# A hybrid attention and retention step: the decay table's load, the order of the output projection's first product, and the place of its row sums are changed

## The chip, the cores and the metric

The kernel runs on one core of a Trainium2 chip. The metric is the device time of one execution in microseconds; a kernel's time is the median of its runs. The engines are named as in the profile: PE is TensorE (matmuls; its weight loads are PEld), DVE is VectorE, ACT is ScalarE, POOL is GpSimd, SP is SyncE. SP, ACT and POOL issue DMAs, each on a queue of its own.

## What is computed

One layer of a streaming encoder, for a prompt of 1024 frames and for 8 running streams of 16 new frames each. All data are float32. Cut to what matters:

```
h = rms_norm(x, norm_pre)                                  # 2048 wide
q_sb|k_sb|v_sb|gate_sb|q_r|k_r|v_r|gate_r = h @ w_in       # 8 parts of 8 heads x 128
# group A, stick-breaking attention, per head, strictly causal
z = q k^T / sqrt(128);  a = sigmoid(z) * prod_{later keys} sigmoid(-z);  o_sb = a v
# group B, retention, per head: rotary q and k, chunks with a decay table `intra`
scores = (q k^T) * intra
o_r = scores v + (q S) * decay_read
S   = S * gamma^n + k^T (decay_write * v)
# merge
y = concat(head_rms_norm(o_sb) * silu(gate_sb), head_rms_norm(o_r) * silu(gate_r))
x = x + rms_norm(y @ w_out, norm_post)
```

The samples attend to a cache of 1024 past keys and values per stream, and start from a given retention state. Keys, values and states are returned as well.

## The kernel before, in words

Every large product is made in two parts per operand: `split` makes a rounded high part (ACT, line 166) and the rest (DVE, line 167), and three matmuls (high x high, high x low, low x high) stand for one.

**Groups and heads.** Frames are handled in two groups: group 0 is prompt tiles 0 to 3 and the samples (640 columns, in pieces of 256 and 384), group 1 is prompt tiles 4 to 7 (512 columns). For each group, `for h in range(H)` goes through eight heads. A head makes its value and gate rows (`rows`, matmuls on line 443) and four column projections (keys and queries of the retention, queries and keys of the attention; matmuls on line 386). The weights come in blocks of 256 KB through tile `wr`.

**Jobs and ticks.** The dependent work of a head is written as generators, the jobs: `ret_branch` (retention), `sb_branch` (attention), `decode` (the samples' attention over the cache), and others. After every matmul of a projection the builder calls `tick()`: a clock advances by one (0.75 for a matmul of the rows), and one job that is due is taken one step further, which issues its next instructions at that place of every engine's order. A job's `yield n` asks for the next step n ticks later. So the constants `D_...` at the top of the file set where a job's instructions stand among the matmuls; where a constant is a pair, the first is for group 0. `drain(job)` runs ticks with no matmul between them until the job is finished. Each engine works through its own order; a scheduler places instructions, and `tied` and `pin` keep a DMA or an operation behind the matmul at which it was written (`tied` in group 0 alone).

**The retention's branch.** `ret_branch` writes the keys (`rk`) to DRAM (`turn_out`, line 629), waits `D_TO` ticks, reads them back in turned blocks into `ro` with four DMAs on SP's queue (`turn_in`, line 636), waits `D_TI` ticks, transposes them on DVE (`rkn`, line 1012), and calls `retention`. That loads the head's decay table `dT` (line 887, 128 KB, SP's queue) and at once makes the first scores: a matmul (line 892), a product with `dT` on DVE (`sc`, line 894), and the matmul with the values (line 910). `dT` has one buffer.

**The attention's branch.** `sb_branch` does its scores per tile of 128 frames (line 742), sigmoids, a running product on DVE (line 672), the turning through DRAM on POOL's queue (`be`), a transposition (line 732), and the product with the values (line 769). Both branches end in `Out.finish`: norm, `turn_out`, `D_TO` ticks, `turn_in` on SP's queue, `D_TI` ticks, transposition on DVE (line 707), gain (708), and the store to a scratch tensor `s_y[group][branch and head]` (709).

**The decode.** `decode` (one per head of group 0) loads eight tiles `kcT` of 512 KB on POOL's queue, `D_ZC` ticks apart, then eight tiles `vc` of 512 KB on SP's queue. The two kinds share six buffers (`V_BUFS`). The value products (line 868) are in two sets of four tiles, `D_VC[1]` ticks apart; between them the last two `vc` tiles are loaded into buffers that the first set freed.

**The output projection** is a Strassen-like scheme of seven products (numbers 1 to 7), each with two halves `nh` of 512 output columns and eight blocks `k` of 128 contraction rows. `weights_of` gives a block's weights, some of them sums that were made ahead (`sum_weights`, scratch `s_b`); `left` and `left_sample` load and split the other operand from `s_y` or from row sums `s_s` (`sum_rows`, run by `sums` with a pace `D_SUM2` or `D_SUM3`). `product` makes one half for the accumulators asked for: two for group 0, two for group 1, one for the samples; `collect` adds the results up. Product 5 of group 0 and the samples comes first, while the last head's branches are still running. Then both branches are drained, the buffers of the first stage are given back, and the second stage begins: group 1's operand of product 1 (`yr`) is loaded, and product 1 runs for both groups, group 0 two blocks ahead of group 1 (`LAG`). The eight row sums of group 1 are made there too (`more`).

Of the kernel before, what the change touches and what calls it, by code (L numbers as in the profile page):

```python
# [11 lines left out]
F32 = mybir.dt.float32  # L12
# [6 lines left out]
P = 128  # L19
D = 2048  # L20
KT = D // P
H = 8
# [14 lines left out]
D_ZP = (2, 2)  # L37
D_Z0 = (19, 11)
D_AV = (9, 11)
D_ZC = 24  # L40
D_ROW = 18
D_VC = (6, 46)
V_BUFS = 6
D_RET = (9, 5)
D_TO = (32, 23)
D_TA = (14, 0)
D_TB = (17, 24)
D_TI = (32, 13)
D_OUT = 4
V_SET = 4  # L50
D_SUM = 6
D_TD = 7
D_OFF = 3
N_READ = 40
D_FIN = 2
D_MR = 6
D_OP = 2
D_SUM2 = (4, 6, 28)
D_SUM3 = (3, 3, 6)
MR = 3  # L60
LAG = 2
AHEAD = 2
HT = KT // 2
HALF = D // 2
# [23 lines left out]
def tile_hybrid_step(  # L88
# [368 lines left out]
    with ExitStack() as s1:  # L457
# [424 lines left out]
            oT = op.tile([P, P], F32, name="doT", tag="doT", bufs=1)  # L882
            Job(out.finish(0, 0, h, 4, oT, s_y[0][h][:, 4 * P : 5 * P]))

        def retention(gi, g, h, out, rq, rk, rkn, rv):
            dT = op.tile([P, 2, P], F32, name="dT", tag="dT", bufs=1)
            tied(nc.sync.dma_start(dT, c_dt[:, h]))

            def scores(i, kind):
                bs = slice(i * P, (i + 1) * P)  # L890
                ps = score_tile("rs")
                nc.tensor.matmul(ps[:, :P], rk[:, bs], rq[:, bs], start=True, stop=True)
                sc = op.tile([P, P], F32, name="sc", tag="sc")
                nc.vector.tensor_tensor(sc, ps[:, :P], dT[:, kind, :], ALU.mult)
                return sc

            S = None
            if gi == 1:
                S = op.tile([P, P], F32, name="S", tag="S", bufs=3)
                nc.sync.dma_start(S, s_S[h])  # L900
            sc = scores(0, 0)
            yield D_RET[phase[0]]
            for i in range(4):
                nxt = None
                if i < 3:
                    nxt = scores(i + 1, 0)
                elif SAMPLE in g["tiles"]:
                    nxt = scores(4, 1)
                po = acc_tile()
                nc.tensor.matmul(po[:, :P], sc, rv[:, i, :], start=True, stop=True)  # L910
# [12 lines left out]
                yield D_RET[phase[0]]  # L923
                pS = score_tile("pS")
                nc.tensor.matmul(pS[:, :P], rkn[:, i, :], rv[:, i, :], start=True, stop=True)  # L925
                Sn = op.tile([P, P], F32, name="S", tag="S", bufs=3)
                if S is None:
                    nc.vector.tensor_copy(Sn, pS[:, :P])
                else:
                    nc.vector.scalar_tensor_tensor(  # L930
                        Sn, S, math.exp(LOG_GAMMA[h] * P), pS[:, :P], ALU.mult, ALU.add
                    )
                S = Sn
                sc = nxt
                yield D_RET[phase[0]]
            nc.scalar.dma_start(s_S[h] if gi == 0 else s_prompt[0, 0, h], S)
            if SAMPLE in g["tiles"]:
                yield from sample_retention(h, out, sc, rq, rkn, rv)
# [62 lines left out]
        def ret_branch(gi, g, h, rows_in, rk):  # L1001
# [2 lines left out]
            rkn = ep.tile([P, 6, P], F32, name="rkn", tag="rkn")  # L1004

            out = Out(nt, "ro")
            s = turn_out(rk[:, : nt * P].rearrange("p (k t) -> p k t", t=P), f"s_rk{gi}_{h}")
            yield D_TO[phase[0]]
            raw = out.o.rearrange("p k d -> p (k d)")
# [6 lines left out]
            nc.vector.tensor_scalar(rkn[:, :4, :], rkn[:, :4, :], dec[:, h, 1:2], None, ALU.mult)  # L1016
            while "rq" not in rows_in:
                yield 3
            yield from retention(gi, g, h, out, rows_in["rq"], rk, rkn, rv)
# [23 lines left out]
        def kept(i):  # L1043
            return [[half[i][:, h // 2, h % 2 * 256 : h % 2 * 256 + 256] for h in range(HT)] for half in mov]

        def first_sample():
            mine["s", 0] = [[half[h // WQ][:, h % WQ, NB_TOK:] for h in range(HT)] for half in mov]
            return left_sample(0, *mine["s", 0], wp, "mr", MR)
# [8 lines left out]
        for gi, g in enumerate(GROUPS):  # L1057
# [6 lines left out]
            for h in range(H):  # L1064
                rows_in = {}

                def rows():
                    if (gi, h) == (1, H - 1):
                        sampled.append(Job(first_sample(), 1))
                    rows_of_head(g, mov, h, None if h else loads)  # L1070
                    if h == 0:
                        nc.sync.dma_start(roots[:, :NB_TOK], s_root)
                        rooted_tables(ropes, g["pieces"])
# [124 lines left out]
            return wh, wl  # L1198

        made = collections.deque()  # L1200
        order_of = iter([(n, nh, k) for n in (5, 1, 2, 5, 3, 6, 7) for nh in range(2) for k in range(HT)] + [(4, 0, k) for k in range(HT)])

        def product(n, nh, groups, sample, ticks, upto=HT, feed=(), lag=0):
            todo = [((g, p), bank(), mine[g, n], TS[p]) for g in groups for p in range(2)]
            if sample:
                todo.insert(2, ("s", bank(), mine["s", SAMPLE_LEFT[n]], TS[0]))
            blocks = []
            for k in range(upto + lag):
                if k < upto:
                    made.extend(load_split(*at) for at in itertools.islice(order_of, AHEAD + 1 - len(made)))  # L1210
                    blocks.append(made.popleft())
                next(iter(feed), None)
                for key, a, x, ts in todo:
                    at = k - lag if key[0] == 1 else k
                    if 0 <= at < upto:
                        times(a, x, at, ts, *blocks[at], at == 0, at == HT - 1)
                        for _ in range(ticks):
                            tick()
            return [(key, a) for key, a, _, _ in todo]

        outs, finishing = {}, {}
# [30 lines left out]
        nxt = Job(left(0, 1, *mine[0, 1], wp, "mr", MR), D_OP)  # L1252
        Job(collect(5, 1, product(5, 1, (0,), True, D_OUT)), 1)
        drain(nxt)
        drain(ret_job)
        drain(sb_job)
        while jobs:
# [2 lines left out]
    with ExitStack() as s3:  # L1260
# [107 lines left out]
                yield 30  # L1368

        (first,) = both(1, G1)  # L1370
        more = Job(sums(fp, [sum_rows(1, h) for h in range(H)], D_SUM3, 3), 30)
        Job(load_gpost(), 40)
        ready = [Job(left_sample(1, *mine["s", 1], fp, "ys", 4), 24)]
        for p in range(4):
            outs[1, p] = rp.tile([P, D], F32, name=f"out{p}", tag=f"out{p}")
        for n, groups in ((1, BOTH), (2, BOTH), (5, G1), (3, BOTH), (6, BOTH), (7, BOTH)):
            for nh in range(2):
                if n > 1 and nh == 0:
                    all_of(ready)
# [166 lines left out]
```

## Time and profile before

| | |
|---|---|
| median of 3 runs | 2297.95 us (2295.87 to 2303.42) |
| the profiled execution | 2302.5 us |
| its span, first to last instruction | 2300.8 us |
| granted TensorE clock, mean | 0.989 |
| PE busy | 2232.6 us (97%), 12002 matmuls |
| DVE, ACT, POOL busy | 1252.0, 908.4, 347.9 us |
| DMA | 462.84 MB, mean 201 GB/s |

Times are microseconds from the start of the span. A row of the timeline has start, duration, engine, line, operation, output and inputs, shape, the count of merged instructions, and in brackets the idle time of the engine before it with what ended it. The profile names for that the last event seen; where that had long been over, it was another, often a DMA. "x4" merges instructions of one kind that follow each other. Rows of windows give, after the stretch and its length, the busy time and count of PE, PEld, DVE, ACT and POOL, then the granted clock, the DMA engines' share and GB/s.

### The profile page before, as it was taken

How to read it: one execution, taken by the hardware profiler on the slowest of the kernel's cores; microseconds unless marked ns; L12 is line 12 of the kernel's file. 1: busy time of each engine (PE TensorE's matmuls, PEld its weight loads, DVE VectorE, ACT ScalarE, POOL GpSimd, SP SyncE). 2: the span in 40 equal slices, each digit the busy share in tenths (PEclk: the TensorE clock that was granted, in tenths of full speed). 3: DMA queues.
4: the chain of work that ended last, by engine and by line, in shares of the span. 5: the costliest groups of instructions: out<-in, count | busy, mean ns of one | idle time of the engine just before them, and what ended most of it. 6: DMA issues, size and time to landing. Idle time of an engine off the chain costs nothing.

```text
span 2300.8 us, 34562 instructions
## 1 busy us (share of the span) xinstructions
PE 2232.6 (97%) x12002; PEld 1896.4 (82%) x12002; DVE 1252.0 (54%) x2692; ACT 908.4 (39%) x1963; POOL 347.9 (15%) x577
## 2 busy tenths in 40 slices
PE   8999899999999999999989999999999999799998
PEld 7888889798888979888768888888888887688886
DVE  5335444354444545446556665756666657456567
ACT  6433232333323333334424343443433445335363
POOL 0022030111202021120202111120212113000020
PEclk9999999999999999999999999999999999899999
DMA  8566566574656658467668887887888757665585
GB/s 283 177 201 187 168 186 192 168 226 156 188 166 184 197 162 237 148 199 244 197 196 225 240 224 236 233 232 220 228 236 234 205 148 196 192 208 187 147 218 175
DMA packets 437743, 462.84 MB, mean 201 GB/s; under 512 B 182336, under 2 KB 298048, under 8 KB 437056
## 3 DMA queue, kind: packets, MB, share of 16 engines
q1 hardware_dynamic: 315328, 300.16, 44.7%
q0 software_dynamic: 28720, 78.41, 12.4%
q10 hardware_dynamic: 93520, 82.07, 11.3%
q8 instruction: 94, 1.54, 0.3%
q14 instruction: 81, 0.66, 0.1%
HBM read 359.58 MB, written 110.36 MB: 204 GB/s over the span
## 4 chain that ended last, share of the span: by engine, by line
PE 83%; DMA 8%; issue 3%; DVE 3%; ACT 2%; SPq 1%; ACTq 0%; DVEq 0%; POOL 0%; POOLq 0%
PE accm L443 34%; PE acc L386 26%; PE a L1177 5%; PE a L1181 5%; PE a L1180 5%; PE pa L769 3%; DMA so<-s_o 2%; PE z L742 2%; PE zc L807 1%; DMA ro<-s_rk 1%; SPq L636 1%; PE pa L910 1%; DMA wr<-w_cols 1%; PE pS L925 1%; PE pd L868 1%
## 5 line engine op out<-in xcount | busy, mean ns | idle before, releaser
L386 PE MATMUL acc<-mh,wh 128*128 128x256 f32 (+2 forms) x1536 | 452.4, 345 | 11.4 <-ACT wh L166 10.4
L443 PE MATMUL accm<-whn,mh 128*128 128x512 f32 x1152 | 453.0, 394 | 1.3 <-DVE qs L1128 1.3
L443 PE MATMUL accm<-wln,mh 128*128 128x512 f32 x1152 | 451.0, 391 | 0.5 <-DVE wln L167 0.5
L443 PE MATMUL accm<-whn,ml 128*128 128x512 f32 x1152 | 450.8, 391 | 0.0
L386 PE MATMUL acc<-ml,wh 128*128 128x256 f32 (+2 forms) x1536 | 446.4, 341 | 0.0
L386 PE MATMUL acc<-mh,wl 128*128 128x256 f32 (+2 forms) x1536 | 445.8, 341 | 0.0
L166 ACT ACTIVATE wh<-wr 128x512 fp32r<-128x512 f32 x376 | 237.0, 633 | 467.6 <-PE acc L386 204.8
L167 DVE TENSOR_TENSOR wl<-wr,wh 128x512 fp32r<-128x512 f32 x376 | 257.3, 688 | 289.3 <-ACT wh L166 276.4
L167 DVE TENSOR_TENSOR wln<-wrn,whn 128x512 fp32r<-128x512 f32 x256 | 175.8, 689 | 311.8 <-ACT whn L166 295.8
L166 ACT ACTIVATE whn<-wrn 128x512 fp32r<-128x512 f32 x256 | 161.3, 632 | 404.5 <-PE accm L443 269.2
L386 PEld LDWEIGHTS acc<-mh,wh 128*128 128x128 f32 x1536 | 283.9, 191 | 32.1 <-ACT wh L166 11.9
L386 PEld LDWEIGHTS acc<-ml,wh 128*128 128x128 f32 x1536 | 286.4, 191 | 21.8 <-issue 3.7
L386 PEld LDWEIGHTS acc<-mh,wl 128*128 128x128 f32 x1536 | 285.9, 191 | 21.8 <-issue 1.2
L443 PEld LDWEIGHTS accm<-whn,mh 128*128 128x128 f32 x1152 | 216.3, 188 | 47.2 <-issue 2.5
L443 PEld LDWEIGHTS accm<-wln,mh 128*128 128x128 f32 x1152 | 216.5, 188 | 44.7 <-DVE wln L167 1.3
L443 PEld LDWEIGHTS accm<-whn,ml 128*128 128x128 f32 x1152 | 216.4, 188 | 44.3
L636 POOL DMA_DIRECT2D be<-s_be x128 | 94.1, 741 | 132.9 <-DMA s_be<-be 110.6
L672 DVE TENSOR_TENSOR_SCAN kp<-kp 128x1152 f32<-128x1152 f32 (+4 forms) x40 | 82.4, 2059 | 37.1 <-POOL kp L661 22.6
L661 POOL TENSOR_SCALAR_AFFINE_SELECT kb<-kb 128x128 f32<-128x128 f32 x64 | 35.8, 572 | 411.8 <-ACT kb L655 410.7
L1177 PE MATMUL a<-wh,mh 128*128 128x512 f32 x240 | 94.2, 393 | 3.1 <-ACT kp L655 2.6
L794 POOL DMA_DIRECT2D kcT<-cache_k x64 | 34.6, 544 | 401.7 <-PE pd L868 207.9
L1181 PE MATMUL a<-wh,ml 128*128 128x512 f32 x240 | 94.1, 392 | 0.0
(265 smaller groups left out, 2974.8 us busy)
## 6 DMA issues: line engine op xcount, KB each, us to landing
wr<-w_cols SPq DMA_DIRECT2D x256, 256.0 KB, 4.4
wrn<-w_rows SPq DMA_DIRECT2D x256, 256.0 KB, 3.6
kcT<-cache_k POOLq DMA_DIRECT2D x64, 512.0 KB, 7.4
vc<-cache_v SPq DMA_DIRECT2D x64, 512.0 KB, 5.1
wr<-s_b SPq DMA_DIRECT2D x80, 256.0 KB, 3.9
br<-w_out SPq DMA_DIRECT2D x64, 256.0 KB, 4.7
s_b<-br ACTq DMA_DIRECT2D x32, 512.0 KB, 5.2
wr<-w_out SPq DMA_DIRECT2D x48, 256.0 KB, 3.6
```

The source lines that it names most:

```text
L166: nc.scalar.activation(hi, src, AF.Copy),
L167: nc.vector.tensor_tensor(lo, src, hi.bitcast(F32), ALU.subtract),
L386: last = nc.tensor.matmul(a[:, :m], lhs[:, j, :], rhs[w][:, j, o : o + m], start=(w == 0 and j == 0 and n == 0), stop=(w == KT // WQ - 1 a ...
L443: anchor[0] = nc.tensor.matmul(banks[t], lhs[q][:, j, ts], rhs, start=(k == 0 and n == 0), stop=(k == KT - 1 and n == 2),)
L636: q.dma_start(raw[32 * i : 32 * i + 32, :].rearrange("p (k a) -> p k a", a=32), s[:, :, 32 * i : 32 * i + 32].rearrange("k (j b) a -> b (k ...
L661: nc.gpsimd.affine_select(blk, blk, pattern=[[-1, P]], base=0, channel_multiplier=1, compare_op=ALU.is_gt, fill=fill,)
L672: nc.vector.tensor_tensor_scan(rev, rev, rev, 1.0, ALU.mult, ALU.bypass)
L742: nc.tensor.matmul(z[:, :c], q2[a][:, i * P : (i + 1) * P], k2[b][:, s : s + c], start=(m == 0), stop=(m == 2),)
L769: nc.tensor.matmul(po[:, :P], at[:, j, :], rest["vn"][j], start=(j == 0), stop=(j == t))
L1177: ins = nc.tensor.matmul(a, hi[k][:, ts], wh, start=first, stop=False)
L1180: nc.tensor.matmul(a, hi[k][:, ts], wl, start=False, stop=False)
L1181: anchor[0] = nc.tensor.matmul(a, lo[k][:, ts], wh, start=False, stop=last)
```

## The change

- The load of `dT` is written in `ret_branch` just before `turn_out` instead of at the start of `retention`.
- Constants: `D_ZC` 24 to 23, `D_VC` (6, 46) to (6, 36), `D_TI` (32, 13) to (36, 13), `D_OUT` (ticks per three matmuls in product 5) 4 to 3, `D_SUM2` (4, 6, 28) to (4, 6, 26).
- Product 1 is made by groups. Its first half for group 0 and the samples follows product 5 in the first stage, ahead of the draining of the branches, with `D_OUT` ticks. Its second half for them comes first in the second stage, while group 1's operand is loaded (`feed`). Then both halves for group 1. Its weight blocks are loaded and split twice; `lag` and `upto` are gone.
- Six of the eight row sums of group 1 (`EARLY`) are made by a job of the last head, `early_sums`, behind the sums that `summed` makes; two stay in the second stage.

```
-D_ZC = 24
+D_ZC = 23
-D_VC = (6, 46)
+D_VC = (6, 36)
-D_TI = (32, 13)
-D_OUT = 4
+D_TI = (36, 13)
+D_OUT = 3
+EARLY = 6
-D_SUM2 = (4, 6, 28)
+D_SUM2 = (4, 6, 26)
-LAG = 2
...
-        def retention(gi, g, h, out, rq, rk, rkn, rv):
-            dT = op.tile([P, 2, P], F32, name="dT", tag="dT", bufs=1)
-            tied(nc.sync.dma_start(dT, c_dt[:, h]))
+        def retention(gi, g, h, out, rq, rk, rkn, rv, dT):
...
             out = Out(nt, "ro")                       # in ret_branch
+            dT = op.tile([P, 2, P], F32, name="dT", tag="dT", bufs=1)
+            tied(nc.sync.dma_start(dT, c_dt[:, h]))
             s = turn_out(rk[:, : nt * P].rearrange("p (k t) -> p k t", t=P), f"s_rk{gi}_{h}")
...
+        def early_sums():
+            while not summed[0].done:
+                yield 4
+            yield from sums(ip, [sum_rows(1, h) for h in range(EARLY)], D_SUM2, 2)
...
                     if (gi, h) == (1, H - 1):
                         sampled.append(Job(first_sample(), 1))
+                        Job(early_sums(), 8)
...
-        order_of = iter([(n, nh, k) for n in (5, 1, 2, 5, 3, 6, 7) ...
+        order_of = iter([(n, nh, k) for n in (5, 1, 1, 2, 5, 3, 6, 7) ...
...
-        def product(n, nh, groups, sample, ticks, upto=HT, feed=(), lag=0):
+        def product(n, nh, groups, sample, ticks, feed=iter(())):
             todo = [((g, p), bank(), mine[g, n], TS[p]) for g in groups for p in range(2)]
             if sample:
                 todo.insert(2, ("s", bank(), mine["s", SAMPLE_LEFT[n]], TS[0]))
+            for k in range(HT):
+                made.extend(load_split(*at) for at in itertools.islice(order_of, AHEAD + 1 - len(made)))
+                block = made.popleft()
+                next(feed, None)
                 for key, a, x, ts in todo:
+                    times(a, x, k, ts, *block, k == 0, k == HT - 1)
+                    for _ in range(ticks):
+                        tick()
...
         Job(collect(5, 1, product(5, 1, (0,), True, D_OUT)), 1)
         drain(nxt)
+        Job(collect(1, 0, product(1, 0, (0,), True, D_OUT)), 1)
         drain(ret_job)
         drain(sb_job)
...
-        more = Job(sums(fp, [sum_rows(1, h) for h in range(H)], D_SUM3, 3), 30)
+        more = Job(sums(fp, [sum_rows(1, h) for h in range(EARLY, H)], D_SUM3, 3), 30)
...
-        for n, groups in ((1, BOTH), (2, BOTH), (5, G1), (3, BOTH), (6, BOTH), (7, BOTH)):
+        Job(collect(1, 1, product(1, 1, G0, True, 2, first)), 1)
+        for _ in first:
+            pass
+        for n, groups in ((1, G1), (2, BOTH), (5, G1), (3, BOTH), (6, BOTH), (7, BOTH)):
...
-                start = dict(feed=first, lag=LAG) if (n, nh) == (1, 0) else {}
-                accs = product(n, nh, groups, n < 4, {1: 2, 7: 2}.get(n, 1), **start)
+                accs = product(n, nh, groups, n in (2, 3), {1: 2, 7: 2}.get(n, 1))
```

More of the change, by code (lines that the diff above doesn't have):

```diff
@@ L1018, in ret_branch @@
                 yield 3
-            yield from retention(gi, g, h, out, rows_in["rq"], rk, rkn, rv)
+            yield from retention(gi, g, h, out, rows_in["rq"], rk, rkn, rv, dT)
             yield from out.finish(1, gi, h, 0, rk, s_y[gi][H + h])
@@ L1200, in tile_hybrid_step @@
         made = collections.deque()
-        order_of = iter([(n, nh, k) for n in (5, 1, 2, 5, 3, 6, 7) for nh in range(2) for k in range(HT)] + [(4, 0, k) for k in range(HT)])
-        def product(n, nh, groups, sample, ticks, upto=HT, feed=(), lag=0):
+        order_of = iter([(n, nh, k) for n in (5, 1, 1, 2, 5, 3, 6, 7) for nh in range(2) for k in range(HT)] + [(4, 0, k) for k in range(HT)])
+        def product(n, nh, groups, sample, ticks, feed=iter(())):
             todo = [((g, p), bank(), mine[g, n], TS[p]) for g in groups for p in range(2)]
@@ L1206, in product @@
                 todo.insert(2, ("s", bank(), mine["s", SAMPLE_LEFT[n]], TS[0]))
[L1207 to L1212, printed above, removed]
-                for key, a, x, ts in todo:
[L1214 to L1218, printed above, removed]
+            for k in range(HT):
+                made.extend(load_split(*at) for at in itertools.islice(order_of, AHEAD + 1 - len(made)))
+                block = made.popleft()
+                next(feed, None)
+                for key, a, x, ts in todo:
+                    times(a, x, k, ts, *block, k == 0, k == HT - 1)
+                    for _ in range(ticks):
+                        tick()
             return [(key, a) for key, a, _, _ in todo]
```

## The prediction

> **What bounds the kernel now.** I read the page first, then the waits of TensorE, then the stretch around each large wait (timeline, windows), then the landing times of the transfers in it.
>
> ```profile
> span 2300.8 us, 34562 instructions
> PE 2232.6 (97%) x12002; PEld 1896.4 (82%) x12002; DVE 1252.0 (54%) x2692; ACT 908.4 (39%) x1963; POOL 347.9 (15%) x577
> ...
> PE pa L910 <- DVE sc L894: 18.0, 8, 5.8
> PE a L1177 <- ACT ah L166: 9.8, 1, 9.8
> PE pa L769 <- DVE kp L732: 5.8, 5, 4.3
> ...
>   PE pa L910: 17.3, 7
> DMA to landing us min/median/max: 3.2/8.6/9.9
> ```
>
> TensorE is busy 97% of the span, and the change takes no matmul away, so what can be won is its idle time (2300.8 - 2232.6 = 68.2 us) and the time that it runs at half clock. The waits (us in total, times, longest) name two places. The last two lines are the answer on the tile dT, cut to 0:1065 us (group 0): 17.3 of the 18.0 us fall there, in seven heads, and the decay table takes 8.6 us to land in the median.
>
> ```profile
> 623.17 1.93 PE L868 MATMUL pd<-vc,kp 128*32 128x256 f32 x32
> 636.09 1.93 PE L868 MATMUL pd<-vc,kp 128*32 128x256 f32 x32
> 637.24 2.20 POOL L794 DMA_DIRECT2D kcT<-cache_k  x4 [11.10 <-PE pd L868]
> 637.67 2.42 SPq L636 DMA_DIRECT2D so<-s_o  x4
> 640.14 3.63 SPq L887 DMA_DIRECT2D dT<-c_dt  x1
> 641.00 0.85 DVE L1012 STREAM_TRANSPOSE rkn<-ro 128x640 f32<-128x640 f32 x1
> ...
> 649.93 0.71 DVE L707 STREAM_TRANSPOSE kT<-so 128x512 f32<-128x512 f32 x1 [3.70 <-DMA wrn<-w_rows]
> 650.88 0.49 PE L910 MATMUL pa<-vv,sc 128*128 128x128 f32 x2 [3.40 <-DVE sc L894]
> ...
> DMA to landing us min/median/max: 2.5/9.9/10.6
> DMA to landing us min/median/max: 2.8/9.7/10.4
> ...
> q0 software_dynamic: 576, 2.10, 54.9%
> q1 hardware_dynamic: 3239, 0.89, 34.7%
> ```
>
> This is head 4 of group 0. The second set of value products (636.09) frees four buffers, and POOL at once loads four cache_k tiles of 512 KB into them (637.24). In 637:649 us they move 2.10 MB on POOL's queue, while SyncE's queue gets 0.89 MB. Under that burst lie the attention's turned rows (so, landing in up to 10.6 us; the ro line below it is the retention's) and dT. VectorE works in order: the transposition L707 sits ahead of L894 and waits for so until 649.93, then L894 runs, and TensorE has stood 3.40 us. The name "wrn" in that row is the last event seen, not the cause: so was issued at 637.67 to 639.2, and 639.2 + 10.6 is 649.8. In head 1 it is dT itself:
>
> ```profile
> 243.39 0.49 DVE L894 TENSOR_TENSOR sc<-rs,dT 128x128 f32<-128x128 f32 x2 [4.29 <-DMA dT<-c_dt]
> 243.74 0.79 PE L910 MATMUL pa<-vv,sc 128*128 128x128 f32 x2 [5.79 <-DVE sc L894]
> 916.49 0.49 PE L910 MATMUL pa<-vv,sc 128*128 128x128 f32 x2 [2.08 <-DVE sc L894]
> ...
> 241.80:248.60 6.80, 4.86 (x19) 4.86 (x20) 3.48 (x8) 2.59 (x6) 0.00 (x0) 0.50 0.79 280
> 385.10:388.50 3.40, 3.40 (x16) 3.40 (x16) 1.67 (x5) 1.43 (x4) 0.00 (x0) 0.50 0.60 161
> ...
> 917.60:921.00 3.40, 3.40 (x16) 3.40 (x15) 1.48 (x4) 1.44 (x4) 0.00 (x0) 0.50 0.31 104
> ```
>
> The windows rows (stretch, TensorE busy first, granted clock third from the end) show a second price: four of the seven stalls are followed by 0.50 clock, the first for 6.8 us and three for 3.40 us (first and last shown). Half of the busy time in them is lost: (4.86 + 3 x 3.40) / 2 = 7.5 us.
>
> ```profile
> 1954.22 0.39 PE L1181 MATMUL a<-wh,ml 128*128 128x512 f32 x1
> ...
> 1958.93 3.55 PE pa L769 x16
> 1973.23 2.02 DMA s_y<-so
> 1975.45 5.12 DMA yr<-s_y
> ...
> 1954.50:1981.20 26.70, 12.10 (x54) 10.06 (x53) 6.42 (x19) 4.03 (x12) 2.18 (x4) 0.83 0.43 126
> 1981.20:2029.80 48.60, 48.60 (x205) 40.09 (x206) 30.02 (x71) 23.84 (x53) 0.00 (x0) 0.95 0.80 262
> ```
>
> The second place is the end of the last branches. Output product 5 ends at 1954.22 + 0.39; the last attention head still has one product to do (L769, 1958.93, after a wait of 4.3 us, the longest of its kind above), then its norm, its turning through DRAM and its store (1973.23); group 1's operand (yr) can only be read behind that, and TensorE stands until 1981.2. In 1954.5:1981.2 it is idle 26.70 - 12.10 = 14.6 us, and product 1 runs to 2029.8.
>
> **The change part by part.** A tick is one step of the planner. First and second set of value products are 46 ticks apart in the order written, and 636.09 - 623.17 = 12.92 us: 0.28 us a tick in group 0.
>
> *Decay table (L887).* One 128 KB load per head on SyncE, no more and no fewer, moved from the retention's start to its opening, D_TO + D_TI = 68 ticks or 19 us earlier, past the turn-out (ACT's queue) and the four turn-ins of ro on SyncE's. It delays those by one issue and 128 KB. 19 us exceed the longest landing (9.9), so dT stops being a cause. Its buffer is free: the last head's retention is drained before.
>
> *D_ZC 24 to 23, D_VC's second 46 to 36, D_TI 32 to 36.* Decode up to its second set of value products took 8x24+18+32+32+7+6+46 = 333 ticks, and takes 8x23+18+32+36+7+6+36 = 319: 14 earlier, 3.9 us. The burst so begins near 633.3 in head 4. L707 and L894 come 4 ticks (1.1 us) later. What lies under the burst hence has 5.0 us more before it is asked for; the stalls of heads 2 to 6 are 3.4 us at most. What is late next: ro, whose fourth turn-in is issued at 637.3 and would now lie under the burst. Its transposition L1012 runs at 641.00; but TensorE only runs dry at 650.88 - 3.40 = 647.48, and L1012 to L894 are some 2 us of work, so ro may be about 4 us late for nothing. The nearer set also wants its last two value tiles 2.8 us sooner, 10.1 us after the first set, hardly more than
>
> ```profile
> DMA to landing us min/median/max: 3.7/5.2/9.3
> ```
>
> their longest landing (answer on vc up to 1165 us): no stall, just. Recoverable are 17.3 + 7.5 = 24.8 us. I leave 0.9 us a head for so and ro, 6.3 us, too short for the clock to drop: **gain 18.5 us** (bounds 24.8, and 8 if two thirds of the stalls stay).
>
> *Product 1 by groups.* Its 10 accumulators x 8 blocks x 3 matmuls stay. Group 0 and the samples (3 of 5 accumulators) go first, one half behind product 5 and one behind the branches' end, 144 matmuls; then group 1. From the windows above, without idle time and half clock the stretch would shrink by 14.6 + 0.05 x 48.6 = 2.4, and by half of the 3.55 us of L769 at 1958.93, 1.8 (sixteen such small matmuls elsewhere take half): 18.8 us. Against it:
> - Its 16 weight blocks are loaded and split twice: 4.2 MB, and on ACT and VectorE
>
> ```profile
> L167 DVE TENSOR_TENSOR wl<-wr,wh 128x512 fp32r<-128x512 f32 x15 | 10.4, 691 | 9.5 <-ACT wh L166 8.1 <-DMA yr<-s_y 1.5
> L167 DVE TENSOR_TENSOR al<-yr,ah 128x256 fp32r<-128x256 f32 x15 | 6.2, 421 | 1.5 <-ACT ah L166 1.5
> 238.00:243.70 5.70, 0.00 (x0) 0.00 (x0) 1.37 (x6) 0.00 (x0) 0.00 (x0) 0.83 1.06 363
> 2000.00:2029.00 29.00, 29.00 (x129) 24.02 (x129) 18.34 (x43) 14.57 (x31) 0.00 (x0) 1.00 0.88 290
> ```
>
>  each. A matmul takes 29.00 / 129 = 0.225 us; group 1's half has 48 of them, 10.8 us. In the second one also product 2's operands are made: VectorE 8 x 0.691 + 16 x 0.421 = 12.3 us; DMA 2.1 + 2.1 MB, 11.6 us at the 363 GB/s of that row, 14.5 us at 290. TensorE waits 0.8 to 3.7 us; I take 2.5, as product 2's last blocks can wait.
> - yr waits for the branches' last store, and on SyncE the weights from group 0's fourth block of the second half on stand behind yr: three blocks are made ahead, 27 x 0.225 = 6 us of cover, against 5.1 us for a load at that place. I take 1 us (0 to 4).
> - The last L769 now lies among product 1's matmuls, and L732 ahead of it behind their splits: 0.5 us (0 to 4.3, the stall of now).
>
> *D_OUT 4 to 3* stretches the branches' ticks in products 5 and 1; the 72 more ticks in product 1's first half take it up: 0, covered by group 0's second half, 16 us; without that cover it is the 9.8 us of now.
>
> *Row sums.* Six of eight go from the stage of products 1 and 2 to the last head: the same loads, four VectorE operations and one store each on ACT's queue. They go behind the weight sums, which end sooner as 28 becomes 26, and VectorE is half idle there. 0.5 us.
> Product 1: 18.8 - 4.5 = **14.3 us**.
>
> *Elsewhere.* The last decode is drained at group 1's first head, where its shorter course saves about 1 us. In group 1 dT is not tied and already early: nothing. D_SUM2 moves the loads of the weight sums (br) against the retention's turn-in; in one head they now fall into its midst:
>
> ```profile
> 1567.01 1.20 SPq L278 DMA_DIRECT2D br<-w_out  x2
> ...
> 1575.01 0.71 DVE L1012 STREAM_TRANSPOSE rkn<-ro 128x512 f32<-128x512 f32 x1 [3.10 <-DMA ro<-s_rk]
> 1576.34 0.80 PE L925 MATMUL pS<-vv,rkn 128*128 128x128 f32 x2 [2.33 <-DVE rkn L1016]
> ```
>
> With the half clock behind it, 3.4 us, that is 4.0 us in one head; it may go or come again: 0, within 4.
>
> **Sum.** 18.5 + 14.3 + 1 = 33.8 us. The profiled execution took 2302.5 us with its 1.7 us around the span, 4.55 above the median of 2297.95. 2302.5 - 33.8 = 2268.7 profiled, **2264 us as a median**.
>
> The rule against the row for the clock: the Trainium skill, TensorE: Matmul & The Clock Gate, section HAM oscillation, wants no idle gap above about 3.4 us and lets shorter ones pass. By that rule only the stalls of 5.79 and 3.40 us would cost clock, 4.1 us and not 7.5, and the median would come out at 2267. The trace differs: 0.50 stands behind a stall of 2.08 us (917.60:921.00).
>
> **The rivals.**
> 1. *The stall changes its name.* The burst now lies on ro, and L1012 waits where L894 did. For it: ro's 9.7 us median landing is already long before the burst touches it. Against it: TensorE's 4 us of slack. Two thirds of the stalls stay, group 0 gives 8: 2297.95 - 23.3 = 2275. The Trainium skill, DMA: Bandwidth & Descriptors, section Queues, rings and completion order, says that each engine takes turns between queues packet by packet; by that rule small rows starve beside big ones wherever the burst lies, and the trace agrees (2.10 against 0.89 MB).
> 2. *Group 1's halves become the bound* through DMA and splits, and the weights stand behind yr: product 1 gives 5. For it: 363 GB/s is as much as any row here shows. 2297.95 - 24.5 = 2273.
> 3. *Slower: the weight sums' loads fall on the turn-in in all seven remaining heads of group 1*, and each costs what head 1 of group 0 paid, 5.79 + 4.86 / 2 = 8.2 us: 57 us, 2264 + 57 = 2321. It decides from (33.8 + 6.9) / 7 = 5.8 us a head. Against it: the meeting above cost 4.0.
> 4. *It doesn't do what it says*: the burst follows other waits of POOL, dT stays late behind blocked loads, and group 1's halves return what idle time gives: 2298.
>
> **How the numbers follow.** Forecast 0.54 (2264, its own range 2255 to 2272), rival 1 0.20, rival 2 0.15, rival 3 0.06, rival 4 0.05. All gains at once, 24.8 + 18.8 + 2 + 4 = 49.6, would give 2248; both rivals 1 and 2 give 2284. The range 2251 to 2288 leaves out rivals 3 and 4 and the last of the best case. Faster by over 0.3% (6.9 us, what a measurement of this kernel can tell): 0.89; within 0.05; slower 0.06.
>
> **What would show it.** In the waits, L910's 18.0 us down to 6 or less, dT landing long before L894, and the cache_k loads some 4 us ahead of their place against the second project of the head. Clock of 1.00 around 242, 385, 651 and 918 us. Between product 5 and group 1's first matmul no wait near 9.8 us, group 0's 144 matmuls in one run. Wrong would make it: L1012 waiting for ro in group 0, TensorE waiting for wh in group 1's halves, or L925 waiting in several heads of group 1.

## The result, and the profile after

| | before | after |
|---|---|---|
| median of 20 runs each | 2299.95 us | 2293.28 us |
| the profiled execution | 2302.5 us | 2289.7 us |
| its span | 2300.8 us | 2288.0 us |

The ratio of the times is 0.9969, with a 95% interval of 0.9961 to 0.9977: the change makes the kernel 6.7 us faster. The prediction had the direction (faster) and not the size: 2264, with a range to 2288, where 2293.3 came out. The two profiled executions differ by 12.8 us, nearly twice what the medians do: the one before lies 2.6 us above its median and the one after 3.6 below. So single stages are compared over several kernels below.

The page after (span and busy time), and TensorE's waits (us in total, times, longest):

```profile
span 2288.0 us, 34700 instructions
PE 2228.4 (97%) x12002; PEld 1889.0 (83%) x12002; DVE 1261.5 (55%) x2708; ACT 920.6 (40%) x1981; POOL 344.2 (15%) x577
...
PE acc L386 <- ACT wh L166: 19.8, 3, 9.4
PE a L1182 <- issue: 6.4, 1, 6.4
PE a L1182 <- ACT wh L166: 4.6, 3, 3.4
PE pa L907 <- DVE sc L891: 2.7, 4, 1.3
```

The retention's lines are now up to 3 lower (910 is 907, 894 is 891, 1012 is 1011) and the product's 1177 is 1182; in the experiments some differ by one or two from these. Of the two waits that the prediction went for, the wait for sc fell from 18.0 to 2.7 us and the 9.8 us wait ahead of group 1's product became 6.4. Two new ones stand beside them: 9.4 us for a weight block (L386) in head 1 and 3.4 us for wh in the product.

Head 4 of group 0, the head shown of before, in the timeline of POOL, SyncE and VectorE:

```profile
631.54 2.14 POOL L794 DMA_DIRECT2D kcT<-cache_k  x4 [9.05 <-PE pd L868]
635.14 6.30 SPq L636 DMA_DIRECT2D so<-s_o  x4
642.56 0.84 DVE L1011 STREAM_TRANSPOSE rkn<-ro 128x640 f32<-128x640 f32 x1 [0.96 <-DMA ro<-s_rk]
...
645.28 0.70 DVE L707 STREAM_TRANSPOSE kT<-so 128x512 f32<-128x512 f32 x1
```

The burst of cache_k starts 5.7 us earlier (637.24 before). The head itself starts 1.8 us earlier (its first rows matmul at 533.99 against 535.76), which leaves 3.9 us, as forecast. L707 finds so landed and has no idle time ahead of it (3.70 before), and the retention's transposition waits 0.96 us on VectorE for ro, which TensorE does not see. That part went as forecast. Head 1 did not. SyncE's queue there, before and then after:

```profile
209.20 1.09 SPq L375 DMA_DIRECT2D wr<-w_cols  x2
...
223.91 4.88 SPq L636 DMA_DIRECT2D ro<-s_rk  x4
228.89 5.79 SPq L636 DMA_DIRECT2D so<-s_o  x4
234.72 0.49 SPq L887 DMA_DIRECT2D dT<-c_dt  x1
235.30 10.51 SPq L375 DMA_DIRECT2D wr<-w_cols  x6
```

```profile
208.67 0.43 SPq L1005 DMA_DIRECT2D dT<-c_dt  x1
215.70 0.33 SPq L375 DMA_DIRECT2D wr<-w_cols  x1
222.57 0.82 SPq L834 DMA_DIRECT2D vc<-cache_v  x2
223.49 5.13 SPq L636 DMA_DIRECT2D ro<-s_rk  x4
228.72 7.91 SPq L636 DMA_DIRECT2D so<-s_o  x4
236.74 9.38 SPq L375 DMA_DIRECT2D wr<-w_cols  x7
...
243.65 2.65 ACT L166 ACTIVATE wh<-wr 128x512 fp32r<-128x512 f32 x4 [10.37 <-DMA wr<-w_cols]
244.33 0.90 PE L386 MATMUL acc<-mh,wh 128*128 128x256 f32 x2 [9.42 <-ACT wh L166]
```

The weight blocks (wr) of the next projection stand behind two vc loads, which wait for their buffers until 222.6, and behind eight turn-ins. Before, two blocks were ahead of these, now one; with the table's load alone (e2, below) it is one as well, at 209.62, behind dT at 208.51. So TensorE runs dry earlier, at 234.9 (237.95 before), and has to wait for blocks issued from 236.74. In the profile before, such blocks were issued from 235.30, right behind dT, and the first landed at 243.88, 0.6 us behind dT; after the change the first lands at 243.62. Head 1's stall had a second cause close behind the one that the profile named, so taking the first away won nothing.

The end of the last branches, after, in windows as shown of before:

```profile
1953.00:1978.00 25.00, 25.00 (x120) 20.78 (x118) 13.14 (x31) 10.80 (x23) 1.53 (x3) 1.00 0.51 152
1978.00:1984.60 6.60, 0.17 (x2) 0.04 (x1) 3.26 (x9) 2.67 (x8) 0.66 (x2) 0.75 0.95 285
1984.60:2011.60 27.00, 25.57 (x96) 18.68 (x96) 17.35 (x38) 15.94 (x36) 0.00 (x0) 0.93 0.80 261
2011.60:2015.20 3.60, 0.20 (x2) 0.05 (x1) 1.77 (x5) 2.91 (x7) 0.00 (x0) 1.00 0.86 246
2015.20:2040.00 24.80, 24.80 (x102) 20.38 (x103) 7.20 (x11) 6.07 (x10) 0.00 (x0) 0.93 0.38 123
```

Group 0's part covers the branch's end without a gap up to 1978.0, and the cover is too short by 6.4 us, because the branch's end now comes later too. The order on VectorE and ScalarE shows one reason:

```profile
1972.75 0.69 DVE L167 TENSOR_TENSOR wl<-wr,wh 128x512 fp32r<-128x512 f32 x1 [1.35 <-ACT wh L166]
1973.36 0.70 DVE L707 STREAM_TRANSPOSE kT<-so 128x512 f32<-128x512 f32 x1
1974.79 0.69 DVE L167 TENSOR_TENSOR wl<-wr,wh 128x512 fp32r<-128x512 f32 x1 [0.73 <-ACT wh L166]
1975.40 0.48 DVE L708 TENSOR_SCALAR so<-kT,gains 128x512 f32<-128x512 f32 x1
...
1974.12 0.63 ACT L166 ACTIVATE wh<-wr 128x512 fp32r<-128x512 f32 x1 [1.41 <-PE a L1186]
1975.91 0.33 ACTq L709 DMA_DIRECT2D s_y<-so  x1
...
1978.41 1.99 SPq L317 DMA_DIRECT2D yr<-s_y  x4
```

The turned rows (so) landed at 1970.2. The transposition L707 and the gain L708 stand behind the splits of group 1's first two weight blocks, and those wait for a buffer that TensorE frees once in 2.04 us. The s_y store comes at 1975.91, and yr is read from 1978.41. That these two splits cost the time is tested in e5.

### The profile page after: what moved, and what is told of

Same layout as the page of the kernel before. It is cut to its first block, busy times and chain, and to the rows that moved or that the text cites. A ratio compares the mean times of both kernels' runs of the same rounds, so it can differ in the third digit from the quotient of the medians.

```text
span 2288.0 us, 34700 instructions
## 1 busy us (share of the span) xinstructions
PE 2228.4 (97%) x12002; PEld 1889.0 (83%) x12002; DVE 1261.5 (55%) x2708; ACT 920.6 (40%) x1981; POOL 344.2 (15%) x577
## 5 line engine op out<-in xcount | busy, mean ns | idle before, releaser
L386 PE MATMUL acc<-mh,wh 128*128 128x256 f32 (+2 forms) x1536 | 444.4, 340 | 19.9 <-ACT wh L166 19.8
L386 PE MATMUL acc<-ml,wh 128*128 128x256 f32 (+2 forms) x1536 | 447.3, 342 | 0.0
L386 PE MATMUL acc<-mh,wl 128*128 128x256 f32 (+2 forms) x1536 | 446.7, 341 | 0.3 <-DVE wl L167 0.3
L166 ACT ACTIVATE wh<-wr 128x512 fp32r<-128x512 f32 x392 | 246.8, 631 | 494.1 <-PE acc L386 159.0
L167 DVE TENSOR_TENSOR wl<-wr,wh 128x512 fp32r<-128x512 f32 x392 | 268.0, 687 | 307.1 <-ACT wh L166 289.6
L167 DVE TENSOR_TENSOR wln<-wrn,whn 128x512 fp32r<-128x512 f32 x256 | 175.6, 688 | 296.0 <-ACT whn L166 291.7
L386 PEld LDWEIGHTS acc<-mh,wh 128*128 128x128 f32 x1536 | 285.1, 189 | 40.3 <-ACT wh L166 20.8
L386 PEld LDWEIGHTS acc<-mh,wl 128*128 128x128 f32 x1536 | 283.0, 189 | 25.2 <-issue 5.8
L386 PEld LDWEIGHTS acc<-ml,wh 128*128 128x128 f32 x1536 | 281.9, 190 | 19.0 <-DVE ml L172 0.4
L661 POOL TENSOR_SCALAR_AFFINE_SELECT kb<-kb 128x128 f32<-128x128 f32 x64 | 31.0, 498 | 437.4 <-ACT kb L655 436.6
L1185 PE MATMUL a<-wl,mh 128*128 128x512 f32 x240 | 94.5, 394 | 0.0
```

What stands on the lines that cost most here:

```text
L166: nc.scalar.activation(hi, src, AF.Copy),
L167: nc.vector.tensor_tensor(lo, src, hi.bitcast(F32), ALU.subtract),
L386: last = nc.tensor.matmul(a[:, :m], lhs[:, j, :], rhs[w][:, j, o : o + m], start=(w == 0 and j == 0 and n == 0), stop=(w == KT // WQ - 1 a ...
L661: nc.gpsimd.affine_select(blk, blk, pattern=[[-1, P]], base=0, channel_multiplier=1, compare_op=ALU.is_gt, fill=fill,)
L1185: nc.tensor.matmul(a, hi[k][:, ts], wl, start=False, stop=False)
```

## Stages over all kernels

From each trace I took the starts of four matmuls (the first on line 550, at 93 to 97 us, the first rows matmul of head 2 and of group 1, and product 5's first) and the end. "Branch" is product 5's first matmul to the last av matmul (attention times values, L769), "gap" from there to group 1's first product matmul, "rest" from there to the end.

| kernel | to head 2 | heads 2 to 7 | group 1 | product 5 to end | branch, gap, rest |
|---|---|---|---|---|---|
| before | 175.7 | 797.3 | 836.8 | 396.3 | 57.8, 19.0, 319.5 |
| after | 178.9 | 784.0 | 836.3 | 394.5 | 63.8, 27.3, 303.4 |
| e1_group0 | 178.7 | 785.2 | 839.7 | 395.5 | 57.1, 18.7, 319.7 |
| e2_table | 181.1 | 784.1 | 840.3 | 396.2 | 57.4, 18.9, 319.9 |
| e3_out | 176.2 | 791.0 | 839.0 | 397.7 | 65.0, 27.2, 305.5 |
| e4_out4 | 178.4 | 784.1 | 837.9 | 398.8 | 66.2, 26.3, 306.3 |
| e5_order | 178.0 | 783.5 | 839.8 | 392.0 | 63.9, 24.6, 303.5 |
| e6_gpost | 178.3 | 784.3 | 837.7 | 390.1 | 62.5, 23.8, 303.7 |
| e7_head1 | 174.3 | 783.0 | 839.2 | 395.5 | 62.5, 27.1, 305.9 |
| e8_sums | 175.6 | 796.7 | 837.4 | 400.3 | 61.2, 20.0, 319.1 |
| e9_nosums | 178.4 | 785.0 | 839.2 | 398.1 | 59.2, 27.6, 311.3 |
| e10_three | 176.0 | 783.4 | 838.9 | 391.6 | 62.3, 22.5, 306.7 |
| e11_three_nosums | 176.4 | 784.3 | 839.7 | 394.1 | 59.6, 25.3, 309.2 |
| e12_group0_head1 | 172.0 | 784.7 | 839.5 | 396.0 | 58.3, 18.8, 319.0 |

## The experiments

The parts of the change alone, and one constant put back; the four shared the runs of before (median 2299.17).

**e1_group0**, before with the first part: the table's load, and

```
-D_ZC = 24
-D_VC = (6, 46)
-D_TI = (32, 13)
+D_ZC = 23
+D_VC = (6, 36)
+D_TI = (36, 13)
```

> Before, with the change's first part alone: the decay table loaded as the job opens, and D_ZC 23, D_VC (6, 36), D_TI 36; group 1 and the output products as before. Theory (group 0 wins about 10 us, the first output product next to nothing): 10 to 12 us faster than before, and group 1's heads shifted by about the same. Rival, as predicted: 17 to 19 us faster, the whole change having lost part of it elsewhere. Second rival: the heads ahead win 10 us but the output products give it back, 0 to 5 us faster.

2294.09 us, ratio 0.9971 (0.9961 to 0.998): 5 to 7 us faster, under the 10 to 12 that I gave and far from the 17 to 19 of the prediction. The output products give nothing back (395.5 us); head 1 does (178.7). It is all that the whole change wins.

**e2_table**, before with the table's load alone, the constants untouched:

```
             out = Out(nt, "ro")
+            dT = op.tile([P, 2, P], F32, name="dT", tag="dT", bufs=1)
+            tied(nc.sync.dma_start(dT, c_dt[:, h]))
```

> Before, with the decay table's load moved and nothing else; the tick constants stay. Theory (in head 1 the weight blocks of the next projection land right behind the table, in heads 2 to 6 the table is the only late one): TensorE's waits for sc go, head 1 wins under 2 us, heads 2 to 6 some 2 to 4 us each, and 6 to 11 us are won in all. Rival (the tick constants do the work, since the bursts still collide): under 3 us.

2292.98 us, ratio 0.997 (0.9959 to 0.9981), as e1 and as the whole change. Heads 2 to 7 take 784.1 us with the load alone and 785.2 with the constants too: the table is the gain, and the shift of the burst by 14 ticks adds nothing that shows. Head 1 loses here as well (181.1 us against 175.7), where I had expected a gain of under 2 us: the total fell into the range that I gave, the reading of head 1 was wrong.

**e3_out**, before with the second and third parts (split of product 1, `D_OUT = 3`, six row sums early), group 0 as before.

> Before, with the change's second part alone: product 1 split by groups, D_OUT 3, the row sums of six heads made in the last head; group 0 as before. Theory (the last branch's end comes later in the split order and group 1's halves run at the pace of the weight blocks): 0 to 5 us faster, and the stretch from the first matmul of product 5 to the end within 4 us of before's. Rival, as predicted: about 14 us faster.

2301.39 us, ratio 1.0011 (1.0 to 1.0022). No gain. Product 5 to the end takes 397.7 us against before's 396.3, within the 4 us that I gave; the gap of 18 to 19 us is now filled with matmuls, and 27 us long.

**e4_out4**, after with `D_OUT = 4`.

> After, with D_OUT back at 4 ticks a key. Theory (the last branch's steps are spread over more matmuls at 3 than at 4, which made its end 6 us late): the last copy of the branch's av comes 4 to 6 us earlier, TensorE's 6.4 us wait ahead of group 1's matmuls shrinks to 0 to 3 us, and 3 to 6 us are won against after. Rival (the branch is held by its loads and splits and not by ticks): no change within 1 us. Second rival: the waits of product 5's second half, which 3 ticks had kept away, come back and it is 2 to 5 us slower than after.

2295.03 us, ratio 0.998 (0.9971 to 0.999), 0.0011 above after's ratio, inside the two intervals. My theory of the ticks falls: the branch's av ends 66.2 us behind product 5's start, later than with 3 (63.8). So the 3 ticks are not what draws the branch out. The wait ahead of group 1 did shrink, to 2.2 us, and others came, as the second rival has it (waits of the last branches' stretch, us in total, times, longest):

```profile
PE a L1182 <- ACT mh L1239: 5.6, 1, 5.6
...
PE a L1182 <- issue: 2.2, 1, 2.2
```

The next four shared another set of runs of before (median 2297.02). Three of them mend one suspected cause each.

**e5_order**, after with two edges in the scheduler's order, without a wait: in the second pass over product 1's weights

```
+            if (n, nh) == (1, 0) and k < 2:
+                turns.append(k)
+                if len(turns) > 2:
+                    behind((low, high)[k], ended[k])   # L708, then the s_y store
```

> After, with one edge more in the order of the queues: the last branch's transpose and scaling (L707, L708) and its s_y store stand ahead of the splits of group 1's first two weight blocks instead of behind them. Theory (the branch's end is not late by its own work but by what the in-order queues of VectorE and ScalarE hold ahead of it): the s_y store 3 us earlier, TensorE's wait ahead of group 1's first product matmul 3 to 4 us instead of 6.4, and 2 to 4 us faster than after, about 2290. Rival (the loads behind the store set the end, not the store): the wait stays within 1 us of 6.4 and the time within 1 us of after's.

2289.16 us, ratio 0.9959 (0.9946 to 0.9972). VectorE's order and the wait:

```profile
1972.43 0.70 DVE L707 STREAM_TRANSPOSE kT<-so 128x512 f32<-128x512 f32 x1
1973.17 0.49 DVE L708 TENSOR_SCALAR so<-kT,gains 128x512 f32<-128x512 f32 x1
...
PE a L1184 <- issue: 3.7, 1, 3.7
```

L708 follows L707 at once, and the wait is 3.7 us instead of 6.4, as expected. Product 5 to the end: 392.0 us, 2.5 under after's. The intervals of the two ratios overlap, so the gain in time alone is not proved; the shorter wait is seen in one trace, at the place of the edit.

**e6_gpost**, after with the output gain's four loads tied behind a matmul of the product:

```
-        Job(load_gpost(), 40)
+        Job(load_gpost(), 112)     # each load waits for the last product matmul written
```

> After, with the four loads of the output gain (1 MB over GpSimd's queue) held until the products of group 1's second half; nothing else. Theory (group 1's halves are bound by what the DMA engines have to bring beside the weights): the yr loads land 1 to 2 us earlier, group 1's halves take 24 to 25.5 us instead of 27.0, and the whole is 2 to 4 us faster than after, or 1 to 3 if the late gain meets product 2. Rival (the splits of ScalarE and VectorE pace the halves, not the loads): halves within 0.7 us of 27.0, no change.

2286.69 us, ratio 0.9951 (0.9939 to 0.9963): 0.0018 under after's, the intervals meeting only at their ends, and 390.1 us from product 5 to the end. The theory was right on yr (wait 2.9 us instead of 6.4) and wrong on the halves: from 1980.9 they run to 2008.2, 27.3 us, no shorter than the 27.0 of after. The gain's loads were in yr's way (its first four loads take 2.1 to 2.6 us to land instead of 5.3 to 5.6), not in the halves'. The late gain then meets product 2's weights, of which four blocks take 6.5 to 7.1 us to land. The wait there is 3.5 us, but it is 3.4 in after and 3.5 in e10, where the gain comes later still, so the gain is not what makes it:

```profile
PE a L1182 <- ACT wh L166: 5.3, 2, 3.5
PE a L1182 <- issue: 2.9, 1, 2.9
```

**e7_head1**, after with so turned in later in head 1:

```
-                yield D_TO[phase[0]]
+                yield D_TO[phase[0]] + (14 if (b, gi, h, at) == (0, 0, 0, 0) else 0)
```

> After, with the turn-in of head 0's branch output (so) 14 ticks later in head 1 of group 0, which puts seven weight blocks ahead of it on SyncE's queue where one stood; nothing else. Theory (in head 1 TensorE waits for weight blocks that stand behind eight turn-ins on the in-order queue): the 9.4 us wait at 244 falls to 0 to 3 us, head 2 starts 6 to 9 us earlier, and the whole is 5 to 8 us faster than after, about 2286. Rival (the burst of cache_k sets when anything lands, in whatever order it is issued): the wait stays over 7 us and the time within 2 us of after's.

2289.36 us, ratio 0.9961 (0.9948 to 0.9975).

```profile
231.05 13.70 SPq L375 DMA_DIRECT2D wr<-w_cols  x7
244.81 2.12 SPq L636 DMA_DIRECT2D so<-s_o  x4
...
241.77 0.90 PE L386 MATMUL acc<-mh,wh 128*128 128x256 f32 x2 [4.19 <-ACT wh L166]
```

Seven blocks now stand ahead of so. The wait falls from 9.4 to 4.2 us, and the stretch to head 2 from 178.9 to 174.3 us. So the order on the queue is a cause, but not all of it: 4.2 us stay, with the blocks issued at 231.05 instead of 236.74. The first of them takes 10.0 us to land, where the block issued ahead of the burst, at 216.13, takes 2.7; so the burst, the rival's cause, very likely has a part too. I expected 5 to 8 us of time and cannot show more than 2 by the ratio.

**e8_sums**, before with the third part alone: `early_sums`, `D_SUM2 = (4, 6, 26)`, two row sums left behind.

> Before, with the third part alone: the row sums of six heads made in the last head of group 1 and two left for the output products. Theory (they lie beside TensorE in both places): within 1.5 us of before. Rival (VectorE and the loads in the last head are the tighter place): 2 to 4 us slower. Second rival (they were in the way of group 1's first product): 2 to 4 us faster.

2306.34 us, ratio 1.0034 (1.002 to 1.0047): slower by about 8 us (5 to 11), twice the price of the slower rival. The trace shows only half of it in the last stage (400.3 us against 396.3); where the rest is, it does not show. TensorE's waits in the last branches' stretch:

```profile
PE pa L770 <- DVE kp L733: 11.5, 2, 10.7
PE a L1184 <- ACT ah L167: 10.8, 1, 10.8
```

The first was 3.7 us in e1. Not the row sums' own loads are in the way: the last of them is stored at 1897, before product 5. The planner steps one job a tick, and with one job more the branch's running product of its third tile (L673, 896 wide) comes 16.1 us behind product 5's start instead of 10.4 in e1, behind a run of retention steps and splits on VectorE. The third and fourth turnings through DRAM then meet. The fourth's store and turn-in on POOL's queue, in e1 and then in e8:

```profile
1926.93 0.90 POOL L629 DMA_DIRECT2D s_be<-be  x1 [1.53 <-DVE or L183]
1932.24 2.35 POOL L636 DMA_DIRECT2D be<-s_be  x3 [4.41 <-DMA s_be<-be]
```

```profile
1931.12 0.90 POOL L630 DMA_DIRECT2D s_be<-be  x1 [0.27 <-DVE so L773]
1940.56 2.35 POOL L637 DMA_DIRECT2D be<-s_be  x3 [8.54 <-DMA s_be<-be]
```

The last store takes 9.0 us to land instead of 4.9, and the turn-in behind it up to 9.8 instead of 5.5. This order of steps is read from one trace of each kernel; I did not move it by itself, so as a cause it is likely and not shown.

The last four, beside runs of before with a median of 2300.18.

**e9_nosums**, after without `early_sums`: all eight row sums in the output products, `D_SUM2 = (4, 6, 28)`.

> After, without the early row sums: all eight heads' row sums in the output products, as before the change. Theory (the row sums' loads and stores in the last head draw out the last branch's turn-ins, which cost 8 us where they were moved alone): the branch's last av ends 60 us or less after product 5's start instead of 63.8, TensorE's wait ahead of group 1's first product matmul is under 4 us, and the time is 2 to 6 us under after's. Rival (the row sums only change places: six more of them in group 1's halves lengthen these): halves of 29 us or more, time within 1.5 us of after's or above. Second rival (the split's matmuls and not the row sums put the branch's end off): the av ends at 62 us or later all the same.

2297.97 us, ratio 0.9986 (0.9977 to 0.9995), slower than after. The branch ends at 59.2 us instead of 63.8 and the wait ahead of group 1 is 2.2 us, as the theory had it; and the first rival takes the gain and more: the row sums' loads now stand in group 1's halves.

```profile
PE a L1181 <- ACT wh L166: 9.5, 4, 3.2
...
PE a L1181 <- issue: 2.2, 1, 2.2
```

The halves take 36.1 us (1983.0 to 2019.1) against 27.0, and the rest from group 1's first matmul 311.3 us against 303.4. So the early row sums cost about 8 us with product 1 as it was (e8), and are worth about 4 with it split (the two intervals touch at one end).

**e10_three**, after with the three mends, the gain's loads at tick 132.

> After, with the three mends together: the order edge of the branch's end, the output gain's loads held back (here until product 2 has begun, 20 ticks later than when alone), and so turned in 14 ticks later in head 1. Theory (the three are apart in place and cause; the first two both shorten one wait of 6.4 us): the wait ahead of group 1's first product matmul 0 to 2 us, head 1's wait 4 us, and 8 to 12 us faster than after, ratio to before 0.992 to 0.9935. Rival (what one mend frees the next stall takes): no better than the best of them alone, ratio 0.995.

2281.80 us, ratio 0.992 (0.9905 to 0.9935): 18 us under before, 11 under after, the lowest median here, with an interval clear of those of before and after.

```profile
PE a L1184 <- ACT wh L166: 7.7, 2, 4.2
...
PE a L1184 <- issue: 1.6, 1, 1.6
```

The wait ahead of group 1 is 1.6 us. Head 1 still waits 6.0 us and group 1's halves wait 4.2 for wh: what the mends free is taken in part by the next weight block.

**e11_three_nosums**, the three mends with the row sums back in the output products.

> The three mends together and the row sums back in the output products. Theory: with the wait ahead of group 1's halves gone already, an earlier branch's end has nothing left to win, and the row sums' loads stand in the halves: 0 to 4 us slower than with the three mends alone. Rival (the row sums in the last head cost whatever follows): 3 us or more faster than with the three mends alone.

2285.82 us, ratio 0.9938 (0.9924 to 0.9951), 4 us slower than e10, at the edge of what the theory gave; the two intervals overlap, so that the early sums still help here is likely and not proved.

**e12_group0_head1**, before with the first part and so later in head 1.

> Before, with the change's first part (table and tick constants) and so turned in 14 ticks later in head 1; output products as before. Theory (the first part wins some 6 us, the mend in head 1 some 4): 8 to 11 us faster than before, ratio 0.995 to 0.9965, and 3 to 8 us slower than the three mends on the whole change, which is what the split is worth once its cover is there. Rival (the split is worth nothing even so): within 1.5 us of the three mends.

2287.94 us, ratio 0.9952 (0.9937 to 0.9966): 11 to 12 us under before with no change at all to the output products; head 1's wait is 2.4 us. e10 lies 6 us below, with intervals that do not overlap: that is what the split, `D_OUT` and the early sums are worth together once e5's and e6's mends bring yr in time.

## Why the prediction was right and wrong

Means of the stages, old code against changed code without mends: to head 2, 175.8 (before, e3, e8) and 178.8 (after, e1, e2, e4, e5, e6, e9); heads 2 to 7, 795.0 and 784.3; group 1, 837.7 (the same three of old code) and 838.9 (all others); product 5 to the end, 396.0 (before, e1, e2, e12) and 395.9 (after, e3, e7). In all -6.6 us, as the 6.7 us of the medians; that they meet to 0.1 us is luck, for single traces of one code differ by several us.

- *Group 0, heads 2 to 7: right.* The sum held 24.8 us less 0.9 a head; without head 1's 8.2 us (5.79 and half of 4.86) that leaves 11.2. Measured: 10.7, closer than the spread of the traces lets one claim. Of the two remedies only one did the work: dT was taken for one cause beside so and the burst, and moving dT alone (e2) does as much as moving the burst too.
- *Group 0, head 1: the first failed step.* "Recoverable are 17.3 + 7.5" took all of head 1's stall as dT's; 7.3 us were to be won and 3.0 were lost. The step counted what the moved load is moved past (ro's turn-ins) and not which weight blocks it pushes behind them. The rows were there: wr x6 issued at 235.30, behind dT at 234.72. e7 and e12 show this by taking about half of the new wait away (9.4 to 4.2 us) and three quarters (8.6 in e1 to 2.4). What stays is very likely the burst's.
- *D_OUT and the cover: the second failed step.* "0, covered by group 0's second half, 16 us" treated the branch's end as something that runs beside the cover. It runs in the same in-order queues as the cover's splits and, after them, those of the next blocks: the gap from the last av to group 1's first matmul grew from 18.9 to 27.3 us (27.2 in e3, 27.1 in e7), and TensorE stood still for 6.4 us of it. Also the branch itself got longer, 63.8 against 57.1 to 58.3 us, of which e9 gives the row sums 4.6. e5 and e6 show the two things that lay between so's landing and yr's: two splits (the wait fell to 3.7 us) and the gain's loads (2.9); both mended, it is 1.6 (e10). The ticks themselves are not at fault: with `D_OUT` back at 4 the kernel is no faster (e4).
- *Group 1's halves: the third failed step, a term too small.* I took 2.5 us for loads and splits and 1 us for weights behind yr. In the profile after: 18.8 recoverable, less 6.4 (wait for yr, the step above), less 5.4 (27.0 us for 96 matmuls of 0.225; 0.07 x 27.0 = 1.9 of it is half clock behind the wait for yr), less 3.4 (wait ahead of product 2), less 1.7 (half clock behind it) leaves 1.9; the two profiles differ by 1.8 in that stage. Rival 2 came true in kind: on SyncE the halves' next weights stand behind yr, and ScalarE then waits for these blocks to land.

```profile
1984.98 2.10 SPq L317 DMA_DIRECT2D yr<-s_y  x4
1987.13 2.77 SPq L1199 DMA_DIRECT2D wr<-w_out  x5
```

Its own losses (5.4, 3.4 and 1.7, 10.5 us) are below its price of 13.8 (18.8 less 5); only with the wait for yr is next to nothing left. What sets the halves' pace stays open: e6 rules out the gain's loads, and no run separates the order on the queue, the DMA engines and the splits.
- *Row sums, "0.5 us": wrong alone and in place, with opposite signs.* About 8 us slower alone, about 4 us faster beside the split (e8, e9). A price found in one order of steps did not hold in the other.
- *"Elsewhere", 1 us of gain:* group 1 and the passage to it are 1.2 us slower, which is within the spread of the traces.
- *Rivals 1 and 3 did not come, but a sign of rival 1 did.* L1011 waits for ro on VectorE in heads 2 to 7 (0.9 to 1.9 us each, next to nothing before); TensorE's only wait above 0.4 us in these heads is 1.35 us, in head 7, so its slack took the rest. In group 1 no head pays what rival 3 asked: the one stall of that kind, 2.33 us before, is 0.9.
- *The base.* 2297.95 was the median of three runs; of twenty it is 2299.95. And one profile is one draw: before has 797.3 us for heads 2 to 7, and with the same code there e8 has 796.7 and e3 791.0.

Errors: head 1 10.3, output products 14.2, passage 2.2, heads 2 to 7 0.5; together 27.2 us, and 2.0 for the base: the 29 us between 2264 and 2293.

## What to carry to other kernels

A stall that the profile puts down to one transfer may have a second late transfer some tenths of a microsecond behind it; before counting the stall as won, look at what lands next on the same queue and at which loads the moved one now pushes behind a blocked one. Work that is to cover a latency covers it only if the steps of that latency do not stand behind the cover's own loads and splits in the in-order queues: put these steps ahead by an explicit order, and hold back bulk loads that nobody needs yet. Price each part of a change alone and in place: here one part cost 8 us alone and won about 4 beside another.

## What was not expected of the hardware

Half clock followed stalls of very different length. Windows of e5 and e6 behind one and the same wait in product 5's first half (1.81 and 1.92 us), and of e6 behind its 2.91 us wait:

```profile
1901.00:1904.40 3.40, 3.40 (x14) 3.01 (x13) 2.03 (x6) 0.83 (x3) 0.10 (x1) 0.51 1.06 287
```

```profile
1900.30:1903.70 3.40, 3.40 (x21) 2.70 (x21) 2.77 (x7) 1.63 (x5) 0.75 (x2) 1.00 1.07 290
1981.90:1985.30 3.40, 3.40 (x10) 2.63 (x9) 2.07 (x7) 1.31 (x4) 0.00 (x0) 0.50 0.97 283
```

Of the first two, the shorter stall was followed by 3.4 us at 0.51 clock and the longer by none. So in these traces a stall near 2 us may or may not cost 1.7 us more; by what, they do not show. The Trainium skill, TensorE: Matmul & The Clock Gate, section HAM oscillation, asks for no idle gap above some 3.4 us, by which shorter ones pass. The two rows at half clock differ, as did 917.60:921.00 in the profile before (a stall of 2.08 us).

And the same code does not stall alike in every execution: heads 2 to 7 took 797.3, 791.0 and 796.7 us in the three traces of the old code and 783.0 to 785.2 in the eleven of the new one. Part of it is the clock: before and e8 have three stretches of 3.4 us at half clock there, e3 has one. A gain read as a sum of stalls in one profile carries some 3 us of that.
